# Sixth product's low part behind a bank's addition, a rounding issued later, and a last product in halves, in a one-core decoder block

## The chip, the cores and the metric

One core of one Trainium2 chip runs the whole block in one launch. The metric is the device time of that launch in microseconds, median of several runs. Names of engines: PE is TensorE's matmul, DVE is VectorE, ACT is ScalarE, POOL is GpSimd, SP is SyncE, which only issues DMAs here.

## What is computed

Sequence 512, width 2048, one layer, all in float32:

```
h  = rmsnorm(x) * g_mix
cb, cc, cv, q, k, v, f, gate_c, gate_a = split(h @ w_in)
conv_branch = (cb * causal_conv3(cc * cv)) @ w_conv_out          # 1024 -> 2048
attn_branch = forgetting_attention(q, k, v, f) @ w_attn_out      # 1024 -> 2048
merged = sigmoid(gate_c + b) * conv_branch + sigmoid(gate_a + b) * attn_branch
x  = x + merged @ w_mix_out                                      # 2048 -> 2048
u  = square(relu((rmsnorm(x) * g_mlp) @ w_ff1))                  # 2048 -> 8192
x  = x + u @ w_ff2                                               # 8192 -> 2048
out = rmsnorm(x) * g_final
```

## The kernel before

**Products.** Nearly every matrix product is cut into two by two blocks and made with seven block products in place of eight, named A11, A12, S1, S3, S2, S4 and A22. S1 to S4 are products of sums of blocks. Each operand in float32 is kept as a high part (rounded by ACT, line 111) and a low part (what the rounding left, subtracted by DVE, line 114). A product is three passes of matmuls: high by high and high by low, alternating, and then the low part of the weights (the tile `tl`) in a pass of its own. So a product can begin when its high part `th` is there and needs its low part `tl` only behind the first two thirds. `th` and `tl` have two buffers each; `places()` hands them out.

**Stages in order of time.** Input projection and attention (to about 860 us), convolution's output projection `conv_out` in four column groups (`Columns`, c = 0 to 3) with the attention's output projection `attn_out` between them (to about 1005), mixing in four column groups g = 0 to 3 (to about 1170), the first MLP product `ff1` in 16 groups (to about 1790), the second, `unit`, in 8 segments of two column halves, and the final norm.

**A group.** A `Group` has four PSUM banks a, b, c and d. `head` makes A11 into a and A12 into b. `tail2` (conv_out, mixing g = 0 to 2) then makes S1 into c, S3 into d, S2 on top of a, S4 on top of c and A22 on top of d. Between them `snap` copies a bank to SBUF (ACT, line 269) and `plus` adds a bank to such a copy (DVE, line 131). The line `half = self.plus(d1, c, self.scale)` of `tail2` adds bank c to the copy of d; S4, the sixth product, writes on c again and so has to wait for that addition. `tail3` (mixing g = 3) has the order S1, S2, S4, S3, A22, and `tail` (ff1) S4, S2, S3, S1, A22, where S1 goes on top of bank a, which `s2 = self.snap(a)` has to have copied first.

**Order.** A planner lays out the instructions of every engine ahead of time, by its own estimates of durations; each engine then runs its list strictly in that order and waits at semaphores. `tc.issue_after(x)` keeps the instructions traced inside it behind x, if they run on x's engine. `keep_in_program_order` and `tied` pin the order further.

**Stored sums.** The squared outputs of ff1 are stored for the second MLP product as seven sums per pair of blocks, with high and low part: in `put_u`, `sums` makes squares on ACT (line 1495), sums on DVE, a rounding of all seven on ACT (line 1511, tile `rh`), a subtraction on DVE (line 1512) and two DMAs by POOL. They are queued in `later` and run by the next group's `tail`; for ff1's group 1 (`late`) that is behind the copy of bank d.

**Extras.** Where a group has `extra` "first", an additional matmul of 192 columns starts the bank ahead of the product's first matmul, which starts it anew: its result is thrown away.

**The end.** The last `unit` (segment 7, second column half) ends with A12 onto bank b and S4 onto bank a for token blocks e = 0 and 1 in turn, 512 columns wide. `finish` adds the bank to the rows (line 1676, DVE) and sums the squares of the result (line 542, ACT). `Final(t)` sums five such parts (line 536, DVE), takes the power -1/2 (line 538, POOL) and scales four column quarters, two on ACT (line 1701) and two on DVE (line 1703), each followed by its DMA out (line 1705).

Of the kernel before, what the change touches and what calls it, by code (L numbers as in the profile page):

```python
# [45 lines left out]
def tile_hybrid_block(ctx: ExitStack, tc, x, g_mix, w_in, b_f, b_gate, conv_w, w_conv_out,  # L46
# [155 lines left out]
    def mm_late(ps, Sx, hi, lo, first):  # L202

        nq = hi.shape[1]
        for qs in (range(nq - 2), range(nq - 2, nq)):
            mm_rows(ps, Sx, hi, lo, first, qs=qs)
# [6 lines left out]
    free, later = [0, 1, 2, 3], []  # L213

    class Group:
# [3 lines left out]
        def __init__(self, view, c1, c2, w, ST, mm, banks, put, scale=1.0, extra={}, after=None, shift=SHIFT):  # L219
# [6 lines left out]
            self.late, self.third = False, False  # L226
# [108 lines left out]
        def tail(self):  # L335
# [17 lines left out]
            d1 = self.snap(d, self.scale)  # L353
            while later:
                later.pop(0)()
# [44 lines left out]
        def tail2(self):  # L400
# [26 lines left out]
            self.put(1, 1, d1)  # L427
            if self.paced:
                with tc.issue_after(half.ins):
                    self.run(c, "S4", X[1, 1], False)  # L430
            else:
                self.run(c, "S4", X[1, 1], False)
# [10 lines left out]
        def tail3(self):  # L443
# [9 lines left out]
            split(X[0, 0], hi, lo)  # L453
# [3 lines left out]
            sub(X[1, 0], X[1, 0], X[0, 0])  # L457
# [778 lines left out]
    def conv_out(c, banks):  # L1236
# [36 lines left out]
        group.after["A12"], group.apart, group.beside = group.two_sums, True, c == 2  # L1273
        if c == 1:
            group.room = lambda i, j: whole_of[c][:, i, :, j, :]
# [215 lines left out]
    def put_u(g):  # L1491
# [5 lines left out]
        def sums(j):  # L1497
# [13 lines left out]
            nc.scalar.activation(out=h, in_=r, func=AF.Copy)  # L1511
# [39 lines left out]
    for g in range(4):  # L1551
# [28 lines left out]
        if g == 3:  # L1580
            group.mid["A22"] = turn_first
            group.freed = lambda: (g0.ahead(1, 1), begin_part("S1", 1))
        group.head(True, between=groups[1].first if g == 0 else lambda: None)
# [79 lines left out]
    ss3 = const.tile([P, NT, 5], F32, name="ss3")  # L1663
    nc.vector.memset(ss3[:, :, 4:5], EPS)
# [9 lines left out]
    def onto_rows(i, j, cg, ps, e, r=None):  # L1674
        t, c, xs = place(i, j, cg, e)
        nc.vector.scalar_tensor_tensor(out=xs, in0=ps[e], scalar=turned[:, t:t + 1] if r is None else r, in1=xs,
                                       op0=ALU.mult, op1=ALU.add)

# [11 lines left out]
    class Final:  # L1690
# [16 lines left out]
        def all(self):  # L1707
            self.columns(0, nc.sync)
            self.columns(3, nc.sync)
            self.columns(1, nc.scalar)  # L1710
            self.columns(2, nc.sync)
# [14 lines left out]
    def unit(seg, cg, ST):  # L1726
# [44 lines left out]
        if end:  # L1771
# [21 lines left out]
            into(1, 1, a, True)  # L1793
            p4 = (main.tile([P, 4, S], F32R, tag="t0", name="th4"),
# [8 lines left out]
            for e in range(2):  # L1803
                mm_rows(b, ST["A12"], *p2, False, blocks=(e,))
                finish(0, 0, cg, b, e)
                mm_rows(a, ST["S4"], *p4, False, blocks=(e,))
                finish(0, 1, cg, a, e)
                Final(e).all()
# [72 lines left out]
```

## Time and profile before

| | us |
|---|---|
| median of 3 runs | 2405.5 (2404.98 to 2408.44) |
| the profiled execution, its own time | 2406.2 |
| its span, first to last instruction | 2404.5 |
| PE busy | 2389.2 |
| DVE busy | 2030.0 |
| ACT busy | 1205.1 |

The span leaves 1.7 us of the execution's own time outside it. Matmuls are pipelined: the end of each is modelled and reaches past the start of the next one, so that a wait in the rows is shorter than the gap between the starts of two matmuls. In a row of the timeline the bracket names the idle time ahead of an instruction and who ended it.

### The profile page before, as it was taken

What the parts mean: (1) busy time and instruction counts of PE and PEld (TensorE: products, weight loads), DVE (VectorE), ACT (ScalarE), POOL (GpSimd) and SP (SyncE); (2) the same over time, 40 slices, a digit from 0 to 9 for tenths busy, and PEclk for the clock granted to TensorE, in tenths of its full rate; (3) what the DMA queues carried; (4) which work ended last, traced back from release to release, by engine and by line L of the source; (5) the groups of instructions that cost most, each with busy time, mean ns of one, the idle gap of its engine ahead of it and who ended that gap; (6) DMA issues with size and microseconds to landing.
All of it is one profiled execution on the core that took longest, in us unless ns stands there. A gap on an engine that the chain in (4) does not pass through costs nothing.

```text
span 2404.5 us, 41377 instructions
## 1 busy us (share of the span) xinstructions
PE 2389.2 (99%) x17778; PEld 2256.0 (94%) x17778; DVE 2030.0 (84%) x1684; ACT 1205.1 (50%) x1240; POOL 288.2 (12%) x459
## 2 busy tenths in 40 slices
PE   9999999999999999999999999999999999999998
PEld 9999999999999999899999999999998888888886
DVE  7987777789888778889988989888897888889898
ACT  7443444445545534456656666665665333333334
POOL 1100111121111102012200000000001001100000
PEclk9999999999999999999999999999999999999999
DMA  8665544565565756566856565665688557665662
GB/s 277 183 191 154 168 145 150 156 204 159 172 207 177 259 191 209 161 210 223 316 192 231 183 232 181 214 213 197 233 303 293 169 196 253 219 217 183 231 231 101
DMA packets 282599, 491.98 MB, mean 205 GB/s; under 512 B 11820, under 2 KB 192136, under 8 KB 282032
## 3 DMA queue, kind: packets, MB, share of 16 engines
q1 hardware_dynamic: 229552, 277.96, 36.5%
q0 software_dynamic: 50096, 206.39, 23.4%
q10 hardware_dynamic: 2768, 4.99, 0.6%
q8 instruction: 139, 2.28, 0.4%
q14 instruction: 44, 0.36, 0.0%
HBM read 379.70 MB, written 109.07 MB: 203 GB/s over the span
## 4 chain that ended last, share of the span: by engine, by line
PE 91%; issue 3%; DVE 3%; ACT 1%; DMA 1%; POOL 1%; SPq 0%; DVEq 0%; POOLq 0%; ACTq 0%
PE a L171 6%; PE a L175 6%; PE a L177 6%; PE d L171 5%; PE d L175 5%; PE a L199 5%; PE a L197 5%; PE a L195 5%; PE d L177 5%; PE c L171 4%; PE c L177 4%; PE c L175 4%; PE d L195 3%; PE d L197 3%; PE d L199 3%
## 5 line engine op out<-in xcount | busy, mean ns | idle before, releaser
L111 ACT ACTIVATE th<-x 128x2048 fp32r<-128x2048 f32 (+1 forms) x280 | 537.0, 1918 | 479.9 <-DVE x L128 162.7
L114 DVE TENSOR_TENSOR tl<-x,th 128x2048 fp32r<-128x2048 f32 (+2 forms) x282 | 639.3, 2273 | 151.9 <-ACT th L111 147.7
L128 DVE TENSOR_TENSOR x<-x,x 128x2048 f32<-128x2048 f32 (+1 forms) x160 | 365.9, 2287 | 23.0 <-DMA x<-in_w_in_dram 18.4
L111 ACT ACTIVATE th<-y 128x2048 fp32r<-128x2048 f32 (+1 forms) x109 | 185.4, 1701 | 273.2 <-PE a L197 138.8
L114 DVE TENSOR_TENSOR tl<-y,th 128x2048 fp32r<-128x2048 f32 (+1 forms) x109 | 219.3, 2013 | 26.7 <-ACT th L111 26.3
L197 PE MATMUL a<-th,us 128*128 128x512 f32 x512 | 199.2, 389 | 0.0
L195 PE MATMUL a<-th,us 128*128 128x512 f32 x512 | 199.2, 389 | 0.0
L171 PE MATMUL c<-S,th 128*128 128x256 f32 x848 | 195.7, 277 | 0.0
L175 PE MATMUL c<-S,th 128*128 128x256 f32 x848 | 195.5, 276 | 0.0
L171 PE MATMUL a<-S,th 128*128 128x256 f32 x784 | 181.5, 278 | 1.0 <-ACT o L269 1.0
L175 PE MATMUL a<-S,th 128*128 128x256 f32 x784 | 180.3, 276 | 0.0
L175 PEld LDWEIGHTS c<-S,th 128*128 128x128 f32 x848 | 159.3, 188 | 0.0
L171 PEld LDWEIGHTS c<-S,th 128*128 128x128 f32 x848 | 159.3, 188 | 0.0
L171 PEld LDWEIGHTS a<-S,th 128*128 128x128 f32 x784 | 147.2, 188 | 1.4 <-ACT o L269 1.2
L175 PEld LDWEIGHTS a<-S,th 128*128 128x128 f32 x784 | 147.3, 188 | 0.2 <-issue 0.2
L199 PE MATMUL a<-tl,us 128*128 128x512 f32 x512 | 136.7, 389 | 0.0
L171 PE MATMUL a<-A,th 128*128 128x256 f32 x544 | 126.6, 278 | 0.0
L171 PE MATMUL b<-A,th 128*128 128x256 f32 x544 | 126.3, 278 | 0.0
L171 PE MATMUL d<-S,th 128*128 128x256 f32 x544 | 126.0, 277 | 0.0
L175 PE MATMUL a<-A,th 128*128 128x256 f32 x544 | 125.5, 276 | 0.0
L171 PE MATMUL d<-A,th 128*128 128x256 f32 x544 | 125.4, 276 | 0.0
L175 PE MATMUL b<-A,th 128*128 128x256 f32 x544 | 125.4, 276 | 0.0
(409 smaller groups left out, 6012.2 us busy)
## 6 DMA issues: line engine op xcount, KB each, us to landing
x<-in_w_in_dram SPq DMA_DIRECT2D x86, 1024.0 KB, 5.9
y<-in_w_ff_dram SPq DMA_DIRECT2D x64, 1024.0 KB, 7.8
x<-in_w_ff_dram SPq DMA_DIRECT2D x60, 1024.0 KB, 8.3
us<-s_d POOLq DMA_DIRECT2D x44, 1024.0 KB, 9.0
s_d<-rh POOLq DMA_DIRECT2D x32, 896.0 KB, 5.3
s_d<-r POOLq DMA_DIRECT2D x32, 896.0 KB, 5.7
x<-in_w_mix_out_dram SPq DMA_DIRECT2D x17, 1024.0 KB, 6.7
g_d<-o POOLq DMA_DIRECT2D x32, 256.0 KB, 3.2
```

Source lines behind the costliest of these rows:

```text
L111: return tied(nc.scalar.activation(out=hi, in_=src, func=AF.Copy))
L114: return tied(nc.vector.tensor_tensor(out=lo, in0=src, in1=hi.bitcast(F32), op=ALU.subtract))
L128: return nc.vector.tensor_tensor(out=out, in0=a, in1=b, op=ALU.subtract)
L171: i = nc.tensor.matmul(o, hi[:, q, js], Sh, start=first and q == 0 and j == 0, stop=False, skip_group_check=True)
L175: nc.tensor.matmul(o, hi[:, q, js], Sl, start=False, stop=False, skip_group_check=True)
L177: i = nc.tensor.matmul(o, lo[:, q, js], Sh, start=False, stop=q == nq - 1, skip_group_check=True)
L195: tied(nc.tensor.matmul(o, Sh, hi[:, q, :], start=begin and q == 0, stop=False, skip_group_check=True))
L197: tied(nc.tensor.matmul(o, Sl, hi[:, q, :], start=False, stop=False, skip_group_check=True))
L199: tied(nc.tensor.matmul(o, Sh, lo[:, q, :], start=False, stop=q == nq - 1, skip_group_check=True))
```

## The change

In `tail2` of conv_out (c = 0 to 3) and mixing (g = 0 to 2) S4's low part is issued behind `half`. In `tail` of ff1's group 1 the parts of S1 are traced ahead of the stored sums, and the rounding `rh` is issued behind S1's high part. In `tail3` the subtraction that makes A22's operand is issued behind S2's low part. Mixing g = 0 gets a 192-column extra ahead of A11 and one ahead of S1. At the end, bank a's second block is added to the rows early, S4 for token block 1 is made in two halves of 256 columns in the two banks of d, each half is added and squared by itself, `ss3` gets a sixth column, and the last column quarter of token block 0 is scaled behind the addition of the second half.

```diff
-    def mm_late(ps, Sx, hi, lo, first):
+    def mm_late(ps, Sx, hi, lo, first, extra=None):
         nq = hi.shape[1]
         for qs in (range(nq - 2), range(nq - 2, nq)):
-            mm_rows(ps, Sx, hi, lo, first, qs=qs)
+            mm_rows(ps, Sx, hi, lo, first, extra, qs=qs)
...
             d1 = self.snap(d, self.scale)
+            if self.late:
+                self.ready["S1"] = hi, lo = self.places()
+                before_sums.append(high_of(X[0, 0], hi))
+                low_of(X[0, 0], hi, lo)
             while later:
                 later.pop(0)()
             self.run(a, "S1", X[0, 0], False)
...
             self.put(1, 1, d1)
+            if self.low_behind:
+                self.ready["S4"] = hi, lo = self.places()
+                high_of(X[1, 1], hi)
+                with tc.issue_after(half.ins):
+                    low_of(X[1, 1], hi, lo)
             if self.paced:
...
             self.ready["S2"] = hi, lo = self.places()
-            split(X[0, 0], hi, lo)
+            low = split(X[0, 0], hi, lo)[1]
             self.half["S4"] = hi, lo = self.places()
             high_of(X[1, 1], hi)
             self.run(a, "S2", X[0, 0], False)
-            sub(X[1, 0], X[1, 0], X[0, 0])
+            with tc.issue_after(low.ins):
+                sub(X[1, 0], X[1, 0], X[0, 0])
             self.done(0, 0)
...
         group.after["A12"], group.apart, group.beside = group.two_sums, True, c == 2
+        group.low_behind = True
...
             h = pf.tile([P, 7, HS], F32R, tag="rh", name="rh")
-            nc.scalar.activation(out=h, in_=r, func=AF.Copy)
+            if before_sums:
+                with tc.issue_after(before_sums.pop().ins):
+                    nc.scalar.activation(out=h, in_=r, func=AF.Copy)
+            else:
+                nc.scalar.activation(out=h, in_=r, func=AF.Copy)
...
+        if g == 0:
+            group.extra = {"A11": "first", "S1": "first"}
+        group.low_behind = True
         group.head(True, between=groups[1].first if g == 0 else lambda: None)
...
+    def finish_half(i, j, cg, ps, e, k):
+        t, c, xs = place(i, j, cg, e)
+        xs = xs[:, k * HS:(k + 1) * HS]
+        made = nc.vector.scalar_tensor_tensor(out=xs, in0=ps[:, :HS], scalar=turned[:, t:t + 1], in1=xs,
+                                              op0=ALU.mult, op1=ALU.add)
+        square_part(xs, ss3[:, t, (c, 4)[k]:(c, 4)[k] + 1], otile([P, HS], "junk"))
+        return made
...
-        def all(self):
+        def all(self, behind=lambda: None):
             self.columns(0, nc.sync)
             self.columns(3, nc.sync)
             self.columns(1, nc.scalar)
-            self.columns(2, nc.sync)
+            made = behind()
+            if made is None:
+                self.columns(2, nc.sync)
+            else:
+                with tc.issue_after(made.ins):
+                    self.columns(2, nc.sync)
...
             into(1, 1, a, True)
+            onto_rows(0, 1, cg, a, 1)
...
-            for e in range(2):
-                mm_rows(b, ST["A12"], *p2, False, blocks=(e,))
-                finish(0, 0, cg, b, e)
-                mm_rows(a, ST["S4"], *p4, False, blocks=(e,))
-                finish(0, 1, cg, a, e)
-                Final(e).all()
+            hi4, lo4 = p4
+            mm_rows(b, ST["A12"], *p2, False, blocks=(0,))
+            finish(0, 0, cg, b, 0)
+            mm_rows(a, ST["S4"], hi4, lo4, False, blocks=(0,))
+            finish(0, 1, cg, a, 0)
+            first = Final(0)
+            mm_rows(b, ST["A12"], *p2, False, blocks=(1,))
+            finish(0, 0, cg, b, 1)
+            def halves():
+                for k in range(2):
+                    w = slice(k * HS, (k + 1) * HS)
+                    mm_rows((None, d[k]), ST["S4"], hi4[:, :, w], lo4[:, :, w], True, blocks=(1,))
+                    made = finish_half(0, 1, cg, d[k], 1, k)
+                return made
+            first.all(halves)
+            Final(1).all()
             return
```

## Rows read from the trace of the kernel before

**Rows 1.** The page: busy time of each engine, share of the span, instructions.

```profile
PE 2389.2 (99%) x17778; PEld 2256.0 (94%) x17778; DVE 2030.0 (84%) x1684; ACT 1205.1 (50%) x1240; POOL 288.2 (12%) x459
```

**Rows 2.** Timeline, conv_out's last group: start, length, engine, line, tiles, [idle before].

```profile
930.52 0.58 ACT L269 ACTIVATE o<-d 128x512 f32<-128x512 f32 x1
...
931.74 1.22 DVE L114 TENSOR_TENSOR tl<-y,th 128x1024 fp32r<-128x1024 f32 x1
...
932.28 1.06 ACT L111 ACTIVATE th<-y 128x1024 fp32r<-128x1024 f32 x1 [1.18 <-PE a L175]
932.87 0.68 DVE L131 TENSOR_TENSOR o<-c,o 128x512 f32<-128x512 f32 x1
...
933.61 0.39 PE L171 MATMUL c<-ys,th 128*128 128x256 f32 x1 [0.47 <-DVE o L131]
```

**Rows 3.** Timeline, mixing g = 2, around the sixth product's start.

```profile
1114.22 0.58 ACT L269 ACTIVATE o<-d 128x512 f32<-128x512 f32 x1
1114.34 2.29 DVE L114 TENSOR_TENSOR tl<-x,th 128x2048 fp32r<-128x2048 f32 x1 [0.48 <-ACT th L111]
...
1115.56 1.07 PE L199 MATMUL a<-tl,M 128*128 128x256 f32 x8
1115.76 1.92 ACT L111 ACTIVATE th<-x 128x2048 fp32r<-128x2048 f32 x1 [0.96 <-PE a L197]
1116.55 0.68 DVE L131 TENSOR_TENSOR o<-c,o 128x512 f32<-128x512 f32 x1
1117.29 0.38 PE L195 MATMUL c<-th,M 128*128 128x256 f32 x1 [0.67 <-DVE o L131]
```

**Rows 4.** Timeline, mixing g = 3, from S2's high part to its low pass.

```profile
1140.83 1.92 ACT L111 ACTIVATE th<-x 128x2048 fp32r<-128x2048 f32 x1 [2.53 <-DVE x L128]
...
1141.26 2.28 DVE L128 TENSOR_TENSOR x<-x,x 128x2048 f32<-128x2048 f32 x1
...
1147.07 4.49 DVE L114 TENSOR_TENSOR tl<-x,th 128x2048 fp32r<-128x2048 f32 x2
...
1149.40 1.20 PE L199 MATMUL a<-tl,M 128*128 128x256 f32 x8 [0.79 <-DVE tl L114]
```

**Rows 5.** Timeline, ff1's group 1, around S1's start.

```profile
1234.57 0.88 DVE L128 TENSOR_TENSOR r<-r 128x256 f32<-128x256 f32 x2
...
1235.53 1.71 ACT L1511 ACTIVATE rh<-r 128x1792 fp32r<-128x1792 f32 x1 [3.05 <-issue]
1237.14 1.89 ACT L111 ACTIVATE th<-x 128x2048 fp32r<-128x2048 f32 x1
1238.94 0.58 ACT L269 ACTIVATE o<-a 128x512 f32<-128x512 f32 x1
...
1239.57 0.38 PE L171 MATMUL a<-S,th 128*128 128x256 f32 x1 [0.95 <-ACT o L269]
```

**Rows 6.** Timeline, PE: a product with an extra, and low passes 512 columns wide.

```profile
888.90 0.25 PE L164 MATMUL d<-ys,th 128*128 128x192 f32 x1
...
891.73 0.28 PE L171 MATMUL a<-ys,th 128*128 128x256 f32 x1
...
2391.56 1.07 PE L199 MATMUL b<-tl,us 128*128 128x512 f32 x4
2394.28 1.10 PE L199 MATMUL a<-tl,us 128*128 128x512 f32 x4
```

**Rows 7.** Timeline, DVE at the end: column quarters, a bank's addition, the last sum.

```profile
2394.73 1.41 DVE L1703 SCALAR_TENSOR_TENSOR x<-x,r,gf 128x512 f32<-128x512 f32 x2 [0.73 <-POOL r L538]
2396.06 0.74 DVE L1676 SCALAR_TENSOR_TENSOR x<-a,turned,x 128x512 f32<-128x512 f32 x1
2397.59 0.16 DVE L536 TENSOR_REDUCE v<-ss 128x1 f32<-128x5 f32 x1 [0.79 <-ACT junk L542]
```

**Rows 8.** One line's instructions, 256 columns: shortest, median, longest in ns; first, last start.

```profile
L1427 DVE SCALAR_TENSOR_TENSOR A<-ptr,cols,A x4: 478/482/486, 1156.6 to 1169.7; 128x256 fp32r<-128x256 f32 x4
...
L542 ACT ACTIVATE junk<-o x32: 370/388/399, 1025.0 to 1175.7; 128x256 f32<-128x256 f32 x32
```

More of the change, by code (lines that the diff above doesn't have):

```diff
@@ L200, in mm_rows @@
                                               skip_group_check=True))
-    def mm_late(ps, Sx, hi, lo, first):
+    def mm_late(ps, Sx, hi, lo, first, extra=None):
         nq = hi.shape[1]
         for qs in (range(nq - 2), range(nq - 2, nq)):
-            mm_rows(ps, Sx, hi, lo, first, qs=qs)
+            mm_rows(ps, Sx, hi, lo, first, extra, qs=qs)
     def moving(t):
         return lambda q: (t[:, 0, q, :], t[:, 1, q, :])
-    free, later = [0, 1, 2, 3], []
+    free, later, before_sums = [0, 1, 2, 3], [], []
     class Group:
@@ L225, in __init__ @@
             self.freed, self.summed, self.paced, self.half = lambda: None, False, False, {}
-            self.late, self.third = False, False
+            self.late, self.third, self.low_behind = False, False, False
             self.nq = view.shape[0] // (2 * P)
@@ L1662, in tile_hybrid_block @@
     x1 = [xp[t // 2][:, t % 2] for t in range(NT)]
-    ss3 = const.tile([P, NT, 5], F32, name="ss3")
-    nc.vector.memset(ss3[:, :, 4:5], EPS)
+    ss3 = const.tile([P, NT, 6], F32, name="ss3")
+    nc.vector.memset(ss3[:, :, 4:], 0.0)
+    nc.vector.memset(ss3[:, :, 5:], EPS)
     NSEG, NW = DFF // 1024, 1024
```

## The prediction

> **What bounds the kernel now.** I read the page first: PE is busy 2389.2 us, 99% of the span of 2404.5 [rows 1], so the kernel is a stream of matmuls, and an edit can gain only where that stream stops, or behind its last matmul. All the inner stops and both ends share the remaining 15 us; 9.1 us of it lie behind the last matmul, which ends at 2394.28 + 1.10 = 2395.38 [rows 6]. DVE is the second engine, at 2030.0 us [rows 1].
>
> Then the timeline of PE, for brackets that name another engine, and around each the timeline of DVE and ACT. Four stops stand where the change works: conv_out's last group [rows 2], mixing g = 2 [rows 3], mixing g = 3 [rows 4], ff1's group 1 [rows 5]. The step between matmuls of 256 columns is 0.113 us: eight of them cover 1.07, seven steps and one length of 0.28 [rows 3, 6]. A bracket is less than a stop costs. The matmul ahead is drawn to its modelled end, 0.28 - 0.11 = 0.16 us past the regular start of the next, and the matmul that waited delays its successor by 0.10 more (0.38 or 0.39 long in place of 0.28). So a stop costs its bracket and 0.27.
>
> **The change part by part.**
>
> *S4's low part behind the bank's addition.* In rows 3 the DVE operation at 1114.34 is S4's own low part, and the addition of bank c, for which PE waits, stands behind it at 1116.55. The copy of bank d that the addition needs ends at 1114.22 + 0.58 = 1114.80. With the order turned the addition runs from 1114.8 to 1115.5 and the low part from there to 1117.8. PE can start S4 at 1115.56 + 8 x 0.113 = 1116.47, so the stop of 0.67 + 0.27 = 0.94 goes. What is late next is the low part: its pass begins 16 x 0.113 = 1.81 later, at 1118.3, so 0.5 us are left. Behind the pair the queue stands as before, for both together are as long as they were. Conv_out's last group is the same picture [rows 2]: low part at 931.74, addition at 932.87, stop 0.47 + 0.27 = 0.74; the copy is done at 931.10. The low part is only 1.22 long there. The other conv_out groups and mixing g = 0 and 1 have the same order and no stop of this kind: nothing. Sum **-1.68**; bounds 0 (the order stays) and -1.68.
>
> *The subtraction behind S2's low part, g = 3.* S2's high part was ready at 1142.75, but DVE took the 2.28 us subtraction at 1141.26 and then small operations, so the low part ran only from 1147.07 [rows 4]. Without it the low part ends at 1149.35 - 2.28 = 1147.1, against 1149.3 - 0.9 (PE's regular arrival, 0.79 + 0.16 ahead of 1149.40, is 1148.45). The stop of 0.79 + 0.27 = **-1.06** goes. But the gain in g = 2 makes PE arrive 0.94 sooner, at 1147.5, and DVE has little idle time between: 0.4 us are left, if DVE's work does not move with PE. The subtraction itself is for the last product and is covered by PE's passes for S4 and S3. Bounds 0 (something else of DVE's list takes the place) and -1.06; I take -1.06, since in the rows that subtraction is the one long piece between.
>
> *The rounding of the stored sums.* ACT stands idle 3.05 us before `rh` at 1235.53, runs S1's high part behind it and only then the copy of bank a at 1238.94, for which PE waits [rows 5]. S1's high part, put first, fits in those 3.05 us (1.89), for S2's high passes, whose buffer it takes over, are long done by then. `rh` starts as before, when the sums end at 1234.57 + 0.88 = 1235.45, and ends at 1237.2; the copy ends at 1237.8, ahead of PE, which is ready at 1239.57 - 0.95 - 0.16 = 1238.46. The stop of 0.95 + 0.27 = **-1.22** goes. What the part adds to DVE is order alone: S1's low part (2.29 us, as in rows 3) may come ahead of the four sums. That is a rival below.
>
> *The two extras.* From an extra to the next product PE takes 891.73 - 888.90 = 2.83 us [rows 6], and 24 matmuls at 0.113 take 2.72: 0.11 each, on the path, for PE has no stop there that would hide it. **+0.23**; bounds 0 (a later stop swallows it) and +0.23.
>
> *The end.* Before, the last addition waits for DVE: the quarters of token block 0 fill it up to 2394.73 + 1.41 = 2396.14, and the addition runs from 2396.06, although PE was done at 2395.38 [rows 6, 7]. From there 0.74 addition, the square of 512 columns, and the last sum at 2397.59 [rows 7]. After, the half behind PE's end needs an addition of 0.48 and a square of 0.39 [rows 8], and the second quarter is out of the way. Against that, the early addition of bank a's second block puts 0.74 on DVE, in a list that is full from there on, and ACT's two quarters may stand ahead of the last square. Three orders, all counted to the last sum (2397.59 before). With both halves ahead of quarters: addition 2395.4 to 2395.9, square and its read-out to 2396.4: -1.2. With the first half ahead and the second behind ACT's quarters, which the 0.74 moves to end at about 2396.8: square and read-out to 2397.3: -0.3. With both behind: +0.3. I take **-0.3**, the middle order, and keep both ends. Matmuls cost nothing here: 512 columns take 2.72 for twelve, 0.227 each [rows 6], twice 0.113.
>
> The Trainium skill speaks against these halves twice. Its page "TensorE: Matmul & The Clock Gate", section "Back-to-back issue gap", gives a sustained 81 ns for 128 columns and 131 ns for 512; by it (an estimate, with some 98 ns for 256) the 24 half-width matmuls would cost 2.35 in place of 1.57, +0.8 us. The trace disagrees: 227 and 113 ns, so this adds nothing. "Advanced Engine Details and Errata", section "The Read-Write Bubble", advises tiles of 512 or more columns for VectorE and ScalarE, since each instruction exposes its latency. Here the trace agrees: half an addition takes 0.48, not 0.37. That is why the third order loses.
>
> **Sum** against the profiled execution (2406.2, its span 2404.5): -1.68 - 1.06 - 1.22 + 0.23 - 0.3 = -4.0, a span of 2400.5 and a time of 2402.2. That execution lies 0.7 above the median of 2405.5, so the forecast for the median is **2401.5 us**.
>
> **The rivals.** What a measurement here can tell from no change is about 0.2%, 4.8 us: the limits are 2400.7 and 2410.3.
>
> Best end: both halves ahead of the quarters (-0.9 more), the extras swallowed (-0.2): 2400.4 to 2400.6. For it: PE finishes the first half 1.4 us before the second. Against: ACT's quarters are traced first.
>
> The halves don't pay: the third order, +0.6 on the forecast, 2402.1.
>
> Given back: DVE's list through mixing's last two groups does not move with PE, and the 0.94 of g = 2 come back as a stop later: 2402.4.
>
> The rounding still in front: DVE takes S1's low part first, from about 1234.4 to 1236.7, then the sums' 1.56, `rh` 1.71, the copy 0.58: 1240.5, 2.1 us behind PE in place of 0.95. That is 1.2 not gained and 0.9 lost: 2403.6.
>
> The order doesn't change: the planner's list stays, and only the extras and the end act: 2405.4. Against it: the low part can't be issued ahead of what it is put behind.
>
> Slower: the addition is now ahead of a low part on a strict list, and it needs ACT's copy of bank d. If ACT makes that copy behind the seventh product's high part, the copy ends at 1115.76 + 1.92 + 0.58 = 1118.3 [rows 3], addition and low part at 1121.2; PE starts S4 at 1119.0 and waits 0.4 once more, some 2.9 us in each of the three mixing groups and by the same count (932.28 + 1.06 + 0.58 + 0.68 = 934.6, against 932.98 [rows 2]) some 1.6 in each of four conv_out groups: 8.7 + 6.5 - 1.68 - 1.06 - 1.22 - 0.1 = +11, 2416.7. It decides from the point where the copy ends 0.5 us later than 1114.80. Against it: in rows 3 the copy stands 1.5 ahead of that high part.
>
> **How the numbers follow.** Forecast 0.41, best end 0.22, halves 0.12, given back 0.08, rounding 0.08, no order 0.04, slower 0.05. Faster by over 0.2%: the best end and a fifth of the forecast, whose time is 0.8 above the limit and whose end may come out 0.9 lower: 0.30. Slower: 0.05. Within: 0.65. The range: 2400.4 less the 0.5 by which runs fell below the median (2404.98), 2399.9; above, the rounding's 2403.6 with the 0.94 given back and halves that don't pay (0.6) on top, 2405.1. It leaves out "no order" and "slower" and some scatter.
>
> **What would show it.** The brackets of rows 2 to 5 gone: bank c's addition ahead of the low part in every conv_out and mixing group, S2's low part of g = 3 about 2.3 us sooner, ACT's idle 3 us filled by S1's high part and bank a's copied before d's last pass ends. From there on each matmul should start as much sooner as was won, to the last, about 3.7 sooner. From last matmul to last sum 2.2 us before, 1.9 after. The prediction is wrong if a new stop stands where one went, above all PE waiting for S4's low part in mixing, or if ff1 and the second MLP product, which had no stops to speak of, show new ones.

## The result, and the profile after

| | before | after |
|---|---|---|
| median, us | 2406.72 (2404.05 to 2410.84, 22 runs) | 2410.19 (2407.4 to 2412.08, 22 runs) |
| ratio to before | | 1.0013 [1.0007, 1.0019] |
| the profiled execution, its span | 2406.2, 2404.5 | 2409.63, 2407.9 |
| last matmul's end | 2395.38 | 2398.43 |

The forecast was 4.0 us sooner; the change is 3.1 us later (0.0013 of 2406.7; 95% interval, in brackets in the table, 1.7 to 4.6). The interval leaves zero out, and the time lies above the whole range of the forecast (2399.9 to 2405.1).

The page's engine row, which answers to [rows 1], says little: PE is busy 1.3 us longer, with 14 matmuls more.

```profile
PE 2390.5 (99%) x17792; PEld 2258.3 (94%) x17792; DVE 2031.1 (84%) x1687; ACT 1205.2 (50%) x1242; POOL 287.8 (12%) x459
```

All four stops of the forecast are gone. The timeline of after, conv_out's last group (answers to [rows 2]; columns as there):

```profile
931.77 0.68 DVE L131 TENSOR_TENSOR o<-c,o 128x512 f32<-128x512 f32 x1
932.37 2.35 DVE L114 TENSOR_TENSOR tl<-y,th 128x1024 fp32r<-128x1024 f32 x2
...
933.01 0.28 PE L171 MATMUL c<-ys,th 128*128 128x256 f32 x1
```

Mixing g = 2 and g = 3 (answer to [rows 3, 4]; all times here are 2 to 4 us later, for a reason that follows):

```profile
1119.48 0.69 DVE L131 TENSOR_TENSOR o<-c,o 128x512 f32<-128x512 f32 x1 [2.08 <-ACT o L269]
1120.09 4.48 DVE L114 TENSOR_TENSOR tl<-x,th 128x2048 fp32r<-128x2048 f32 x2
...
1120.92 0.28 PE L195 MATMUL c<-th,M 128*128 128x256 f32 x1
...
1148.25 2.28 DVE L114 TENSOR_TENSOR tl<-x,th 128x2048 fp32r<-128x2048 f32 x1
...
1151.49 1.07 PE L199 MATMUL a<-tl,M 128*128 128x256 f32 x8
...
1152.25 2.29 DVE L128 TENSOR_TENSOR x<-x,x 128x2048 f32<-128x2048 f32 x1
```

And ff1's group 1 (answers to [rows 5]):

```profile
1235.09 1.90 ACT L111 ACTIVATE th<-x 128x2048 fp32r<-128x2048 f32 x1
1238.23 1.71 ACT L1524 ACTIVATE rh<-r 128x1792 fp32r<-128x1792 f32 x1 [1.24 <-issue]
1239.85 0.58 ACT L269 ACTIVATE o<-a 128x512 f32<-128x512 f32 x1
...
1241.68 0.28 PE L171 MATMUL a<-S,th 128*128 128x256 f32 x1
```

The addition stands ahead of the low part; the subtraction at 1152.25 stands behind S2's low part; S1's high part at 1235.09 fills ACT's idle time, of which 1.24 of 3.05 is left. None of the four matmuls has a bracket. The loss is elsewhere, in mixing g = 1, ahead of A22. Timeline of PE, after:

```profile
1078.20 1.07 PE L199 MATMUL c<-tl,M 128*128 128x256 f32 x8
1084.47 0.58 PE L195 MATMUL d<-th,M 128*128 128x256 f32 x1 [5.20 <-ACT th L111]
1084.85 0.41 PE L197 MATMUL d<-th,M 128*128 128x256 f32 x1
...
1087.59 0.28 PE L195 MATMUL d<-th,M 128*128 128x256 f32 x1
```

PE stands for 5.20 us for A22's high part on ACT, and then its matmuls are 0.41 long instead of 0.28, 0.21 apart, until 1087.59. The windows of after show why (start:end, length, busy time and instructions of PE, PEld, DVE, ACT, POOL, granted clock, DMA share, GB/s): the clock was granted at 0.50, the lower of its two levels (1.2 GHz), behind the stop.

```profile
1070.00:1079.00 9.00, 9.00 (x82) 9.00 (x81) 4.31 (x5) 1.80 (x4) 2.40 (x4) 1.00 0.95 304
...
1084.20:1087.50 3.30, 3.03 (x14) 3.04 (x15) 2.61 (x2) 3.27 (x7) 0.71 (x1) 0.50 0.47 171
```

What ACT did meanwhile is in its timeline, before:

```profile
1077.13 0.63 ACT L111 ACTIVATE staged<-f 128x512 fp32r<-128x512 f32 x1 [5.81 <-DMA h_d<-staged]
1077.79 0.33 ACTq L1446 DMA_DIRECT2D h_d<-staged  x1
1078.16 1.92 ACT L111 ACTIVATE th<-x 128x2048 fp32r<-128x2048 f32 x1 [0.40 <-ACT staged L111]
1080.33 0.84 ACT L1430 ACTIVATE f<-ptr,cols 128x256 f32<-128x256 f32 x2 [0.25 <-DMA h_d<-f]
```

and after:

```profile
1078.50 0.63 ACT L111 ACTIVATE staged<-f 128x512 fp32r<-128x512 f32 x1 [7.20 <-DMA h_d<-staged]
1079.16 0.33 ACTq L1457 DMA_DIRECT2D h_d<-staged  x1
1080.74 0.84 ACT L1441 ACTIVATE f<-ptr,cols 128x256 f32<-128x256 f32 x2 [1.61 <-DMA h_d<-f]
1081.47 0.63 ACT L111 ACTIVATE staged<-f 128x512 fp32r<-128x512 f32 x1
1081.99 0.60 ACT L269 ACTIVATE o<-a 128x512 f32<-128x512 f32 x1
...
1082.51 1.91 ACT L111 ACTIVATE th<-x 128x2048 fp32r<-128x2048 f32 x1
```

Before, A22's high part (1078.16) ran between two instructions that each wait for a store of finished blocks to `h_d` to land, to have its buffer back. After, it stands behind both, and behind another rounding and a copy. An order on ACT that the diff doesn't touch has turned, and ACT had its buffer back from the first of the two stores 1.4 us later as well (in four executions of the kernel before, unchanged, that moment scatters by 1.6 us, from 1076.59 to 1078.19).

How far after is ahead of before (minus) or behind it (plus), in the starts of the first matmul of the same product, taken from the two timelines, the difference at 902.7 set to zero; later_end is the last experiment below:

| product | before's time | after | later_end |
|---|---|---|---|
| conv_out's last group, A22 | 936.46 | -0.76 | 0 |
| mixing g = 0, A11 | 1004.73 | -0.25 | -0.02 |
| g = 0, A22 | 1044.74 | -0.85 | -0.02 |
| g = 1, S4 | 1074.40 | -0.76 | -0.02 |
| g = 2, S3 | 1105.17 | +4.72 | -0.04 |
| g = 3, A22 | 1164.52 | +2.59 | -1.41 |
| ff1 group 1, A22 | 1245.13 | +2.17 | -2.66 |
| last matmul's end | 2395.38 | +3.02 | -2.63 |

### The profile page after: what moved, and what is told of

It is laid out like the page before. It is cut to its first block, busy times and chain, and to the rows that moved or that the text cites. A ratio compares the mean times of both kernels' runs of the same rounds, so it can differ in the third digit from the quotient of the medians.

```text
span 2407.9 us, 41407 instructions
## 1 busy us (share of the span) xinstructions
PE 2390.5 (99%) x17792; PEld 2258.3 (94%) x17792; DVE 2031.1 (84%) x1687; ACT 1205.2 (50%) x1242; POOL 287.8 (12%) x459
## 4 chain that ended last, share of the span: by engine, by line
PE 94%; DVE 2%; DMA 1%; issue 1%; ACT 1%; POOL 0%; SPq 0%; DVEq 0%; POOLq 0%; ACTq 0%
PE a L171 6%; PE a L175 6%; PE a L177 6%; PE a L195 6%; PE a L197 6%; PE a L199 6%; PE d L171 5%; PE d L175 5%; PE d L177 5%; PE c L171 4%; PE c L175 4%; PE c L177 4%; PE d L195 3%; PE d L197 3%; PE d L199 3%; PE b L171 3%
```

## Experiments

Each run stands beside runs of the kernel before on the same chip; the ratio is to those, and 0.001 is 2.4 us. Edits are to the changed kernel ("after") or to the kernel before, as said.

**Group 1's low part left out, alone, and with A22's high part put first on ACT again.** no_g1 is after with

```diff
-        group.low_behind = True
+        group.low_behind = g in (0, 2)
```

> All of the change, but in mixing g = 1 S4's low part is left where the kernel before has it (g = 0 and 2 keep it behind the addition). Theory (order on ACT): in g = 1, and there alone, the low part behind the addition made the planner put A22's high part behind two copies f, a rounding and the copy of bank a, which wait for stores of h_d; that gave the one new stop of 5.4 us ahead of the seventh product and 3.4 us at half clock, some 1.7. Without it both go and the rest stays: 3.5 - 7.0 = -3.5 us against the kernel before, ratio 0.9985. Rival (extras): the two extras of g = 0 shift the stores, the stop stays at 3 us or more and the time stays within 1 us of the changed kernel. Rival (stores): the store that ACT waits for lands 1.4 us later than before (1078.4, before 1077.0) whatever ACT's order: a stop of 1.4 to 2.7 stays, the time is 0.8 to 2.2 below the kernel before.

Measured: 2408.38, 0.9999 [0.999, 1.0008]. ACT has before's order and the stop is 0.19 long. The loss is gone, but of the gain that was expected nothing shows: other stops came, which a later part tells of.

only_g1 is before with that one line for g = 1.

> The kernel before with one edit: S4's low part behind the addition in mixing g = 1. Theory (order on ACT): the same stop ahead of the seventh product of g = 1, 4 to 5.4 us, and TensorE at the lower of its two clock levels behind it for about 3.4 us, 1.7 more: +5.7 to +7 us, ratio 1.0024 to 1.0030. Rival (extras): it needs the two extras of g = 0 to show: within 1 us of the kernel before.

Measured: 2411.2, 1.0015 [1.0007, 1.0024], +3.6 us, less than the 5.7 to 7 expected; in its profile PE ends 5.09 later. Within the intervals one reordered low part costs what the whole change lost, and the row is after's:

```profile
1086.08 0.58 PE L195 MATMUL d<-th,M 128*128 128x256 f32 x1 [5.38 <-ACT th L111]
```

copies_behind is after, low part still behind the addition, but the two copies `f` ahead of A22's high part are issued behind it (its low part moves up on DVE with it):

```diff
+            if copies_later:
+                self.ready["A22"] = hi, lo = self.places()
+                high, low = split(X[1, 0], hi, lo)
+                with tc.issue_after(high.ins):
+                    copies_later.pop()()
...
+            copies_later.append(copies) if (g, i, j) == (1, 0, 0) else copies()
```

> All of the change, the low part behind the addition in all three groups; in mixing g = 1 the two copies f of the first quarter are traced behind A22's high part and issued behind it. Theory (order on ACT): A22's high part is again the first thing behind the rounding that waits for the store, about 1.5 to 4 us sooner. If the order alone was at fault the stop is under 0.5 us, there is no half clock, and the time is that of the kernel without the low part behind in g = 1, -3.5 us against the kernel before. Rival (stores): the rounding itself still waits for a store that lands at 1078.4, the high part ends at 1080.9 and PE, there at 1079.0, stops for about 1.9: -1.6 us if the clock stays. Rival (low part itself): the stop is where it was, 5.4.

Measured: 2407.59, 1.0 [0.9991, 1.0009], level with the kernel before and sooner than after, but not the 1.6 or 3.5 us below before that were expected. In the timeline of PE

```profile
1081.73 0.39 PE L195 MATMUL d<-th,M 128*128 128x256 f32 x1 [1.58 <-ACT th L111]
```

with the clock granted at 1.00 behind it. So ACT's order is worth 5.20 - 1.58 = 3.6 us of stop and the stretch at half clock; the 1.58 that stays is the store, whose buffer ACT got at 1078.73. The order on ACT turned in both variants that put the low part behind the addition in g = 1 and leave ACT's list to the planner (after and only_g1), and in none without it. Which estimate in the planner turns it was not tried.

**The other early parts, one at a time.** Each is before with one part of the diff: only_conv (conv_out's four groups), only_g0 (mixing g = 0), only_extra (the two extras).

```diff
# only_conv
+        group.low_behind = True
# only_g0
+        group.low_behind = g == 0
# only_extra
+            group.extra = {"A11": "first", "S1": "first"}
```

> The kernel before with one edit: S4's low part behind the addition in conv_out's four groups. The stop at 932.9 goes (0.63 by the starts of matmuls). Theory (mixing's first two groups wait for transfers): PE enters mixing 0.6 us sooner, and by the seventh product of g = 1 (1080 in the kernel before), which waits for a store that ACT's rounding needs, the 0.6 are lost: 0 to -0.2 us. Rival (the gain stays): -0.6 us at every matmul behind it to the end. The times can't tell the two apart, the starts of the matmuls can.

> The kernel before with one edit: S4's low part behind the addition in mixing g = 0. That low part is the last reader of its block of weights, and the load of the next block into the same buffer is issued when it ends (1037.64 and 1037.67 in the kernel before). Theory: the load is issued 0.7 us later, at 1038.3 to 1038.4, with its subtraction, addition and the product on bank b in g = 1 behind it by a fixed 5.9 us behind the landing: a stop of 0.3 to 1.7 us at 1050.7, by whether the load takes 6.0 or 7.5 us; +0.3 to +1.7 us. Rival: 0, the load has 0.7 us to spare.

> The kernel before with one edit: the two 192-column extras ahead of A11 and S1 in mixing g = 0. Forecast of the change: 0.11 us each, +0.2. It also moves two roundings of merged sums on ACT and three short operations on DVE ahead of or behind low parts in g = 0. Theory: 0 to +0.3 us, no new stop over 0.3 us in g = 0. Rival (the extras are what brings the stops in g = 1): a stop of 1 us or more at 1050.7 or 1080, +1 us or more.

Measured: 2406.64, 1.0 [0.9991, 1.0009]; 2407.77, 1.0003 [0.9994, 1.0012]; 2408.06, 1.0 [0.9991, 1.0009]. None moves the time, and for conv_out and the extras that is not because nothing was won.

only_conv is 0.76 ahead at 936 and level at 1004. Some 0.6 of it went at 950, in `attn_out`, where before has no stop:

```profile
950.66 0.50 PE L520 MATMUL pt<-act,tl 128*128 128x512 f32 x1 [0.31 <-DVE tl L114]
```

The block of weights behind that `tl` was requested at the same time (934.79, before 934.72) and landed 1.7 later (943.93 against 942.24). ACT waits for it (timeline of only_conv):

```profile
944.04 1.92 ACT L111 ACTIVATE th<-raw 128x2048 fp32r<-128x2048 f32 x1 [5.48 <-DMA raw<-in_w_attn_out_dram]
```

In before that line stands at 942.35 with 3.15 of waiting. A transfer that lands by its own time takes the gain back: in all six runs with conv_out's edit 0.35 to 1.54 us are lost between 936 and 1005. Scatter of the landing has a part in it, for only_g1, without that edit, has the same stop at 950 and loses 0.75; the other twelve without it lose at most 0.1.

only_extra was to be 0.23 slower; it is 0.87 ahead of before by 1044.74. The timeline grouped by line and form, PE, 1016 to 1027 (busy time, mean ns | idle), shows before

```profile
L197 PE MATMUL c<-th,M 128*128 128x256 f32 x16 | 4.0, 281 | 0.0
```

and only_extra

```profile
L197 PE MATMUL c<-th,M 128*128 128x256 f32 x16 | 3.8, 276 | 0.0
```

and the windows of before and of only_extra over the same 11 us

```profile
1016.00:1027.00 11.00, 11.00 (x96) 11.00 (x95) 10.70 (x11) 5.66 (x9) 1.80 (x3) 1.00 0.05 18
```

```profile
1016.00:1027.00 11.00, 11.00 (x100) 11.00 (x99) 10.73 (x11) 4.92 (x8) 1.99 (x3) 1.00 0.07 23
```

PE is 100% busy at a granted clock of 1.00 in both, but the one makes 100 matmuls where the other makes 96: the starts are 0.1133 us apart in one and 0.1178 in the other. Before runs at the slower step through most of mixing g = 0; an extra at its head brings the quicker one. That is so in every profile: between 1004 and 1045 the eight kernels with the two extras make 187 to 280 of some 340 steps at 0.1133, the twelve profiles without them one at most. At 1080 the gain is lost again. The timelines of ACT and PE of only_extra:

```profile
1077.65 0.63 ACT L111 ACTIVATE staged<-f 128x512 fp32r<-128x512 f32 x1 [6.97 <-DMA h_d<-staged]
...
1080.65 0.39 PE L195 MATMUL d<-th,M 128*128 128x256 f32 x1 [1.20 <-ACT th L111]
```

PE comes 0.6 sooner and finds the same store not landed. How much is lost there scatters: the same matmul starts up to 1.3 us apart in the four profiles of before. only_g0's own stop (it was expected at 1050.7, from a load of weights requested later) was 0.08 long: that expectation was wrong.

**The stores and DVE behind them.** In no_g1 PE is 1.35 ahead at 1044.74 and 2.11 behind at 1105.17. Its timeline of PE names three stops in between:

```profile
1051.29 0.38 PE L195 MATMUL b<-th,M 128*128 128x256 f32 x1 [1.67 <-DVE o L131]
...
1081.31 0.39 PE L195 MATMUL d<-th,M 128*128 128x256 f32 x1 [0.19 <-ACT th L111]
...
1095.31 0.66 PE L1432 MATMUL ptr<-ident,o 128*128 128x128 f32 x4 [1.39 <-DVE o L1415]
```

The first goes back to a load of w_mix_out, issued at 1037.88 (before 1037.67) and landed at 1045.42 (1044.36). The last waits at the end of a chain of DVE work without a gap. give_later is before with the last part of g = 0's finished blocks handed out behind A22's high part of g = 1:

```diff
-            for n, part in (("A12", "S1"), ("S1", "S3"), ("S2", "A22")):
+            for n, part in (("A12", "S1"),) if g == 1 else (("A12", "S1"), ("S1", "S3"), ("S2", "A22")):
...
+                def last_part(before=before):
+                    with tc.issue_after(groups[1].high.ins):
+                        before.give("S3", "A22")
```

> The kernel before with one edit that the change does not have: in mixing g = 1 two stores of the group before (parts S3 and A22) are traced behind the seventh product and issued behind its high part, so that ACT no longer waits for the store that lands at 1077.0 before it makes that high part. Theory (the seventh product of g = 1 is set by this store): the high part ends 3 us sooner or more, at 1077 or earlier, and PE goes from the sixth product to the seventh without the stop of 0.2 us (0.3 to 1.5 in the other runs): -0.3 to -0.5 us if nothing stops later, and what is gained ahead of 1080 is no longer lost there. Rival: the wait moves to the copies f behind it and to the product on bank b at 1093: 0 or more.

Measured: 2408.36, 1.0006 [0.9997, 1.0015]. The stop at 1080 is gone, and the same work on DVE makes new ones of 1.50 at 1085.5 and 2.67 at 1093.4 (each counted as start to start less the regular step).

before_ns and change_ns take the ten stores of mixing g = 0 away, from before and from no_g1, so that ff1 reads part of a weight there and its result is not the block's:

```diff
+                if g == 0:
+                    return
```

> The kernel before without the ten stores of h_d in mixing g = 0 (what ff1 reads there is put in place at about 300 us from a part of a weight, so that part of the result isn't computed). Theory (mixing's g = 1 waits for these stores): ACT makes the seventh product's high part 3 us sooner, the stops at 1079.8, 1082.0 and 1092.6 (0.20 + 0.38 + 0.77) shrink to 0.3 together: -1 us against the kernel before. Rival: loads or DVE hold g = 1, the stops stay: 0.

> The change without the low part behind the addition in g = 1, and without the same ten stores. Theory (what is won ahead of 1080 is lost to the stores): nothing is lost there now, and conv_out's 0.7, the extras' 0.9, and 0.7, 0.9 and 1.1 of the three later edits all stay: -4.3 us against the kernel before without these stores (-5 against the kernel before). Rival (loads of weights and DVE hold g = 1 as well): a stop of over 1 us at 1050 or 1093, -2 to -3 against the kernel before without the stores.

Measured: 2411.22, 1.0019 [1.0011, 1.0028], and 2406.84, 1.0002 [0.9993, 1.0011]. The copy that fills `h_d` instead ran at the kernel's start and made the first product 4.4 us later in both, so only their difference counts: 4.4 us. In both the stops between 1079 and 1093 are gone (one of 0.31 is left in change_ns), so the stores are what PE waited for there. But by the profiles 2.7 of it lie in ff1, where before_ns runs at the slower step; by 1093 change_ns is only 0.43 ahead. What the early edits would be worth without the stores is thus not settled.

**The three later edits alone**, later_three: before with the low part behind the addition in g = 2, the order in `tail3` and the later rounding.

```diff
-            group.extra = {"A11": "first", "S1": "first"}
-        group.low_behind = True
+            group.extra = {}
+        group.low_behind = g == 2
```

(and conv_out's line and the end as before.)

> The kernel before with the three edits that lie behind mixing's second group, and nothing ahead of it or at the end: S4's low part behind the addition in mixing g = 2, the subtraction behind S2's low part in g = 3, the rounding of the stored sums later in ff1 group 1. Without the low part in g = 1 the change as a whole came out level with the kernel before, although the stops at 932.9, 1116.3, 1148.3 and 1238.3 were gone: a stop of 1.9 us stood at the first addition of g = 1 (bank b's start, 1049.3) and one of 1.6 at 1093.6. Theory (early edits cost it): mixing's first two groups wait for transfers, and what the change moves ahead of them lost what the later three win; by themselves these win 0.73 + 0.94 + 1.12 = 2.8 us: ratio 0.9988. Rival (given back everywhere): the stops only mark where PE meets DVE and the transfers; taken away, they stand elsewhere: within 0.5 us of the kernel before.

Measured: 2404.95 (2404.47 to 2406.68), 0.9992 [0.9983, 1.0001], -1.9 us, with an interval that just holds 1. By starts of products it wins 0.73 in g = 2, 0.94 in g = 3 and 1.11 in ff1, and has a longer stop at 1093.7 (1.40 against 0.77).

later_extras is later_three with four extras each in g = 2 and 3, where before runs at the slower step for a part of the time.

```diff
+        if g in (2, 3):
+            group.extra = {"A11": "first", "A12": "first", "S1": "first", "S3": "first"}
```

> The kernel with the three later edits alone, and 192-column extras ahead of A11, A12, S1 and S3 in mixing g = 2 and 3. The traces show two steps between matmuls of 256 columns, 0.1133 and 0.1178 us, both at the full granted clock and with PE shown 100% busy; a stretch keeps one of them for 10 to 70 us and changes it at a stop or at an extra. With the two extras in g = 0 alone PE was 0.93 us sooner by 1044, against +0.22 by the forecast's price. In the kernel with the three later edits 1096 to 1168 is all at 0.1178, some 2.9 us. Theory (an extra brings the quicker step back): after most of the eight extras the step is 0.1133, 1 to 2.5 us of the 2.9 go, less 8 times 0.07: -0.5 to -2 us against the three edits alone, -2 to -3.5 against the kernel before. Rival (each extra costs 0.11): +0.9 against the three alone.

Measured: 2405.42, 0.9994 [0.9985, 1.0003]. Steps at 0.1178 in mixing fall from 1083 to 527, which is 2.5 us, but stops (the extras with them) grow from 5.69 to 7.48, with new ones of 0.84 at 1113.6 and 0.75 at 1164.0: nothing is left.

**The end in a written-out order**: ACT squares the first half, scales quarter 0, squares the second half, scales quarter 1; DVE adds both halves, scales quarter 3, makes the last sum, scales quarter 2. no_g1_end3 is no_g1 with it, later_end is later_three with it and the halves.

```diff
+            made, squared = half(0)
+            with tc.issue_after(squared().ins):
+                zero = first.columns(0, nc.sync)
+            made, squared = half(1)
+            with tc.issue_after(zero.ins):
+                last_square = squared()
+            with tc.issue_after(made.ins):
+                first.columns(3, nc.sync)
+            with tc.issue_after(last_square.ins):
+                first.columns(1, nc.scalar)
+            second = Final(1)
+            with tc.issue_after(reduces[-1].ins):
+                first.columns(2, nc.sync)
+            second.all()
```

> As the change without the low part behind in g = 1, and at the end an order written out: on ACT the first half's square, token block 0's first quarter, the second half's square, its second quarter; on DVE both halves' additions, a quarter, the last sum, the other quarter. Theory: the halves paid nothing (last sum 2.20 us behind PE's last matmul, 2.21 before) because both squares stood behind both of ACT's quarters. In the order written out the second addition runs 0.1 to 0.6 behind PE's end, its square behind one quarter: last sum 1.5 us behind PE's end, 0.7 us less than without this order, so -4.2 us against the kernel before. Rival: the transfers out, not the last sum, set the end: 0 to -0.2.

> The three later edits (g = 2, g = 3, ff1 group 1) and the end with the order written out, nothing else of the change. Theory: -1.7 as the three alone, and from the last matmul to the last landing 7.8 us in place of 8.1: -2.0 us against the kernel before, ratio 0.9992, and none of its executions with the slower step behind 1240, since no stop is left there: all within 2.5 us of the fastest.

Measured: 2405.45, 0.9994 [0.9985, 1.0003], and 2403.83 (2402.02 to 2405.35), **0.9991 [0.9982, 0.9999]**. later_end is the one version here whose whole interval lies below the kernel before, by 2.2 us by the ratio. Among fifteen versions an upper end of 0.9999 alone would say little, but nine of its eleven times lie below the lowest of the 33 of before beside it (2404.68). That all would lie within 2.5 us of the fastest was wrong (3.3). The timeline of after at the end (answers to [rows 7]):

```profile
2397.53 0.48 DVE L1702 SCALAR_TENSOR_TENSOR x<-d,turned,x 128x256 f32<-128x256 f32 x1
...
2398.34 1.33 ACT L1729 ACTIVATE x<-x,r 128x512 f32<-128x512 f32 x2 [0.26 <-POOL r L548]
...
2399.01 0.48 DVE L1702 SCALAR_TENSOR_TENSOR x<-d,turned,x 128x256 f32<-128x256 f32 x1
...
2399.58 0.40 ACT L552 ACTIVATE junk<-x 128x256 f32<-128x256 f32 x1
...
2400.09 0.42 ACT L552 ACTIVATE junk<-x 128x256 f32<-128x256 f32 x1
...
2400.63 0.16 DVE L546 TENSOR_REDUCE v<-ss 128x1 f32<-128x6 f32 x1 [0.48 <-ACT junk L552]
```

and of later_end:

```profile
2392.69 0.48 DVE L1702 SCALAR_TENSOR_TENSOR x<-d,turned,x 128x256 f32<-128x256 f32 x1 [0.46 <-PE d L199]
...
2393.30 0.40 ACT L552 ACTIVATE junk<-x 128x256 f32<-128x256 f32 x1
...
2393.82 0.16 DVE L546 TENSOR_REDUCE v<-ss 128x1 f32<-128x6 f32 x1
```

In after both half squares stand behind ACT's two quarters (2398.34, 1.33 for the pair), and the last sum comes 2.20 behind the last matmul's end (2398.43), as before (2.21). The last transfer lands 8.14 behind the last matmul in both. In later_end the last sum comes 1.17 behind it (2392.65 to 2393.82), but the last landing 7.84: of that 1.0, 0.3 arrives. Some 0.4 goes at POOL's power behind the last sum (0.92 long in place of 0.55), and 0.3 at the last transfer, which lands 3.73 behind its issue in place of 3.39. no_g1_end3 has the same 1.16 and 7.82.

**All that looked good together**: best is later_three with g = 0's extras, give_later's edit and the written-out end; best_x adds later_extras.

> The three later edits, the two extras of g = 0, the stores of g = 1 traced later (as in the run beside it), and the end with the order written out; no low part behind an addition in conv_out or in g = 0 and 1. Theory: the extras' 0.9 are no longer given back at 1080, three later edits 1.7, the end 0.3: -2.9 us against the kernel before, ratio 0.9988. Rival (transfers and DVE hold mixing's g = 1 and 2 whatever ACT does): the extras' 0.9 are lost at 1093: -2.0.

> The kernel of the run beside it with extras ahead of A11, A12, S1 and S3 in mixing g = 2 and 3 too. Theory (an extra brings the quicker step back): another -0.5 to -2 us, -3.4 to -4.9 against the kernel before. Rival (each costs 0.11): +0.9 against the kernel of the run beside it.

Measured: 2405.93, 0.9997 [0.9988, 1.0006], and 2406.15, 1.0 [0.9991, 1.0008]. best is 1.4 ahead at 1086 and loses it in one stop of 2.55 at 1091.6, where PE waits for DVE.

**The kernel before, unchanged, three times more**, to see what a difference of one profile is worth.

> The kernel before, unchanged, for a second profile. Three runs whose code of ff1 is that of the kernel before stood at the slower step of 0.1178 us from about 1240 to 1308 (2.7 us); the profile of the kernel before did not. Theory (chance decides after a stop): its eleven times fall in two groups, 2405 to 2407 and 2408 to 2410, and the profile shows the slower step behind 1240 if its time is in the upper one. Rival (the edits do it): the quicker step in any case, and a stop at 1093 under 1 us.

> The kernel before, unchanged, third profile. Chance: in some executions of it the step behind the stop at 1238 is 0.1178 us, and then the time is 2408 or more (a quarter of its times are). Edits: 0.1133, as in the two profiles so far, and 2404 to 2407.

> The same, fourth profile: by chance one of the two shows the slower step with a likelihood of about a half; by the edits neither does.

Measured: 2405.8 (2404.93 to 2409.12, 1.0 [0.9991, 1.0009]), 2409.84 and 2405.35. The stop of g = 3 was 1.43, 2.59 and 0.98 long, against 0.95 in the profile of the forecast. before_look2 took over 2408 with the quicker step in ff1, which neither expectation had. In it the clock fell behind that stop, the mean granted being 0.91 and 0.79 in two stretches from 1150 to 1160: (1 - 0.91) x 3.4 + (1 - 0.79) x 6.5 = 1.7 us on top. Its timeline of PE:

```profile
1151.54 1.18 PE L199 MATMUL a<-tl,M 128*128 128x256 f32 x8 [2.43 <-DVE tl L114]
```

and its windows:

```profile
1150.00:1153.40 3.40, 1.86 (x14) 1.87 (x14) 3.40 (x2) 2.46 (x7) 2.36 (x4) 0.91 0.96 286
1153.50:1160.00 6.50, 6.50 (x48) 6.50 (x48) 3.45 (x4) 4.02 (x4) 2.01 (x3) 0.79 0.96 316
```

later_three and later_end, without that stop, keep to narrower ranges (2404.47 to 2406.68 and 2402.02 to 2405.35) than before does (2404.05 to 2410.84). But no_g1 and no_g1_end3, whose edits take the same stop away, do not (2405.53 to 2410.80 and 2403.56 to 2409.13), so it is not shown that the stop makes the scatter.

None of the four profiles of before shows the slower step of 0.1178 in ff1 between about 1228 and 1308, where after, copies_behind, no_g1_end3, only_conv, only_g0, only_extra and before_ns show it and lose 1.6 to 3.0 us there (350 to 680 matmuls, 0.0045 each). The last four of these seven have ff1's code unchanged. no_g1 and no_g1_end3 have the same instructions in the same order on PE, DVE, ACT and POOL up to the end of the kernel, and only the second shows it: no edit ahead of ff1 is needed for it. Chance from one execution to the next would do it; that it alone does is not shown.

## Why the prediction was wrong

**The step that failed** is one sentence of the first part: "The other conv_out groups and mixing g = 0 and 1 have the same order and no stop of this kind: nothing." It looked for a stop to remove, and took a place without one as free. In g = 1 the edit turned another engine's list, and that cost a stop of 5.20 and a stretch at half clock: from -0.76 to +4.72 in the table. only_g1 reproduces it by itself, and copies_behind, with that high part first on ACT again, takes 3.6 us of stop and the half clock away. The trace of before had the warning, in rows that the forecast didn't read: A22's high part at 1078.16 stands between two waits for stores on a strict list, and PE needed it right behind its end, at 1080.13. The rival "slower" looked at the right engine, but for the opposite order: bank d's copy behind the seventh product's high part, with PE waiting for S4. That did not occur. What came is that high part behind other copies, with PE waiting for A22, in one group. It is not the whole miss: without it, in no_g1, the change measures 0.9999 [0.999, 1.0008], not the 4.0 us sooner of the forecast.

**The low part's own terms held**: forecast -0.74 and -0.94, measured -0.76 and -0.95 in after. But the 0.74 of conv_out did not last: 0.5 of it was gone by 1004.73. This is the second step that failed, "From there on each matmul should start as much sooner as was won, to the last", with a rival only for DVE's list in g = 2 and 3. The rows showed the give-back at transfers instead, at 950, 1050 and 1080, and at DVE's full list at 1093. In g = 2 and 3 of after no wait for DVE took a gain back; the 0.7 lost there between 1153 and 1165, to the slower step and two stops of 0.1 and 0.2, is about what stretches at the quicker step had won in those groups before.

**The subtraction** was forecast at -1.06 and measured at -1.15 in after and -0.94 in later_three and later_end. The worry that the 0.94 of g = 2 would use up its 0.4 us of slack did not come true. In later_end g = 2 gave 0.54 only: the stop went there too, but 0.25 was lost just ahead of it, in S2's second half. The stop of g = 2 has no fixed length in before either: four profiles show 0.83, 0.47, under 0.2 and 0.35.

**The rounding** was forecast at -1.22, measured by S1's start at -0.91 in after and -1.12 in later_end (the 0.1 of the next matmul comes on top), in the order foreseen: S1's low part stayed behind the sums, so the rival fell. In after some 0.2 is missing because the product ahead of S1 ran at the slower step: its 48 matmuls took 0.0045 longer each (sixteen low ones cover 2.05 at 1239.80 where later_end's cover 1.98). The stop in before varies too (1.12, 0.29, 1.09, 0.94).

**The extras** had the wrong sign: forecast +0.23, measured -0.6 in after and about -0.9 in only_extra by 1044.74. The term took 0.113 as the step everywhere, from one product at 888.90 [rows 6] and the low passes of [rows 3]; in mixing g = 0 it was 0.1178. And the premise above it, "an edit can gain only where that stream stops, or behind its last matmul", falls with it: a stream without a stop was 4% too slow, and could gain.

**The end** was forecast at -0.3 by the middle order. The outcome is the third, "halves don't pay": both squares behind the quarters, last sum at 2.20 behind the last matmul against 2.21, last landing at 8.14 in both. So the halves were worth nothing, and the third order's price of +0.3 was too high. The span's end lies 9.5 behind the last matmul in place of 9.1, but these 0.4 stand behind the last landing and are not the edit's: only_conv, whose end is unchanged, has them too (9.5). What the "best end" promised is nearly there if the order is written out, 1.0 to the last sum, but only 0.3 of it arrives.

**What no term had** is 0.85 between ff1's group 1 and the last matmul. Its windows show 505 matmuls where before makes 515 in the same 58 us of ff1:

```profile
1242.00:1300.00 58.00, 58.00 (x505) 58.00 (x503) 49.44 (x39) 36.07 (x39) 2.65 (x5) 1.00 0.58 203
```

Put together, by the profiles: conv_out -0.76, given back +0.51, extras -0.60, on to g = 1's S4 +0.09, g = 1 and the start of g = 2 +5.48, the rest of g = 2 and g = 3 -2.13, ff1's first two groups -0.42 (with -0.91 of the rounding in it), the slower step +0.85, behind the last landing +0.4: +3.4, against the spans' 2407.9 - 2404.5.

## What to carry to other kernels

An edit that moves one instruction in a planned order is priced by the order that comes out on every engine, not by the wait that it removes: leave it out where no wait pays for it, and read the lists of the other engines around each place where it acts, above all a needed instruction that stands next to one waiting for a DMA. A gain ahead of a transfer that lands by its own time lasts only up to it: edits behind the last such place (here g = 2, g = 3 and ff1) kept most of what they won, those ahead of it next to nothing. Where an engine is 100% busy, count its instructions in equal windows: the step between them can differ at the same granted clock.

## What the hardware showed that was not expected

Matmuls of 256 columns have two steps at a granted clock of 1.00, 0.1133 and 0.1178 us. Each is kept for long: the slower for 68 us from 1240 in only_extra, the quicker for 545 us from 1240 in before. The step changes mostly at stops, at the seams between products and at the extras of 192 columns; what sets it is open. The Trainium skill's page "TensorE: Matmul & The Clock Gate", section "Back-to-back issue gap", gives the gap of an isolated matmul by the number of columns, which is 109 ns for 256 at the full clock; both steps here are longer, by 4% and 8%.

The same transfers land at different times from one execution to the next: ACT had its buffer back from the store in g = 1 at 1077.13, 1077.25, 1078.19 and 1076.59 in the four profiles of before, and at 1077.65, 1078.50 and 1078.73 in only_extra, after and copies_behind. The DMA share over 1070 to 1079 was 0.94 in before and 0.95 in after. A stop that such a landing ends is not a constant of the kernel.
